# A decoder layer on one core: the last 32 prompt tokens of the first half move from the row gathers to the dense expert products, and three early products move behind the gates' table

## The chip, the cores and the metric

The kernel runs on one core of a Trainium2 chip. The metric is the device time of one execution in microseconds (us); the median of three timed runs stands for the kernel.

## What is computed

One decoder layer for a prompt of 1024 tokens and 8 sample sequences of 4 tokens, which share all weights. The mixer (a state-space scan and dilated window attention) and the first norm are not touched by the change. What follows them is:

```
h   = LayerNorm1(ALPHA * x + m)
out = LayerNorm2(ALPHA * h + PEER(h))

qh  = h @ w_q                               # 8 heads, two halves of 128 each
s1, s2 = qh[:128] @ keys_1.T, qh[128:] @ keys_2.T
top 16 of s1, top 16 of s2, then the top 16 of their sums  -> 128 experts e of 16384, gates g
hid = gelu(u_tab[e] . h)
out = sum over the 128 experts of g * hid * v_tab[e]
```

Each token uses 128 of 16384 experts; each of the tables u and v holds 16384 rows of 1024 numbers (64 MB).

## The kernel before

**Two ways to the experts.** The prompt is worked through in two halves of 512 tokens (`PARTS`, line 36); the 32 sample tokens go with the first half through the mixer. The experts are then computed in two ways that run beside each other:

- *By row.* The 512 tokens of the first half (`TD`, line 37) lie in four tiles of 128 tokens. For each tile, each of the two tables and each of the 128 chosen experts, `gathers` (line 1851) fetches one row per token with an indirect DMA that POOL issues (line 1866, 128 rows of 4 KB), and VectorE (DVE) multiplies it: line 1892 for u (a dot product with the token), line 1897 for v (an accumulation into a bank pair of PSUM). That makes 1024 such steps. Six row buffers are in use and the fetch runs five steps ahead (`ROWS, LOOK`, line 66). A tile ends with its norm (`norm2`, line 1905), two loads of the norm's vectors, two POOL instructions and a store.
- *Dense.* For the 512 tokens of the second half and the 32 sample tokens (`TE` = 544, line 38) `dense` (line 1674) computes all 16384 experts: 128 products with u (a "hidden" product: gelu, then the gate is multiplied in) and 128 with v (an "output" product, added to the result). Expert rows come in 16 blocks `c` of 8 products `k`, per block first the 8 hidden ones, then the 8 output ones. A product is a `step` (line 431) of 48 matmuls: 8 pieces of the depth, three part products each (high by high, low by high, high by low part of 32-bit numbers), and two column pieces `TPC` (line 62), here 288 and 256 wide. Each product takes 0.5 MB of weights, loaded in two halves by SP, split by ScalarE (ACT, line 370) and POOL or DVE (line 371) two products ahead.

**The gates' table.** The dense way needs the gate of each (expert, token) pair. `gates` (line 1596) builds it four tokens at a time: DVE compares (line 1631), POOL multiplies (line 1633), PE does four 128x128 products (line 1640), ACT copies the result out of PSUM (line 1650), and SP stores 32 tokens at once to DRAM (line 1652). The table of 544 tokens takes 136 such groups. The 32 sample tokens come first: their experts are known already (`given`, line 1602). The other four tiles wait until the choice of experts for the second half (the lane `top`, DVE work in `route`) is done; the first of them then runs its `choose` on DVE and POOL in one go (lines 1665 to 1669).

**The order of the work** is written out by hand. A product calls `tick` a set number of times, and at each tick every lane (the choice of experts, the gates' table, the gathers) advances by its rate, so that its instructions stand between those of the products on each engine. 16 hidden products (`BEFORE`, line 93: the eight of block 0 and two each of blocks 1 to 4) are computed early, while the table is built, with `EARLY` ticks each (line 89); those of blocks 1 to 4 are parked in DRAM (line 1721) from two buffers `er` and fetched back later. In this stretch the gathers advance by `GATHERT` = 0.2 steps per tick. All 16 use the same PSUM room, so that each waits for the gelu of the one before.

After the 16 products the table's lane is finished off, its memory is closed, SP loads the first two pieces of the table (`table`, line 1687; issued in line 1694), and DVE multiplies the gates in (`weigh`, line 1701). The other 240 products follow with `DTICKS` = 4 ticks each; the steps by row that are left are spread evenly over them (line 1823). The last two products run one column piece after the other, and the norm of the dense tokens (`cnorm`, line 1291) ends the kernel.

Of the kernel before, what the change touches and what calls it, by code (L numbers as in the profile page):

```python
# [7 lines left out]
F32 = mybir.dt.float32  # L8
# [3 lines left out]
AF = mybir.ActivationFunctionType  # L12
ALU = mybir.AluOpType
# [6 lines left out]
NB = 8  # L20
# [12 lines left out]

PARTS = [(0, 512, True), (512, 512, False)]
TD, PD = PARTS[-1][:2]
TE = PD + NS
NTG = TD // 128
NPAIR = 50  # L40
PACK = NE * NE
# [44 lines left out]
NLO = "vpvpvpvp"  # L86


EQ, OBUFS, EARLY = 4, 4, [8] + [9] * 13 + [4] * 2


AHEAD = {1: 2, 2: 2, 3: 2, 4: 2}
BEFORE = [(0, 0, k) for k in range(8)] + [(c, 0, k) for c in AHEAD for k in range(AHEAD[c])]
STEPS = [s for s in ((c, half, k) for c in range(NE // 8) for half in range(2) for k in range(8)) if s not in BEFORE]


# [45 lines left out]
def layout(inp):  # L142
# [59 lines left out]


OUTS = {
    "y": (TD, D),
    "y1": (128, 8, TE),
    "pk": (128, 4, SEQ + NS),
    "pv": (128, 4, SEQ + NS),
# [9 lines left out]
def unlayout(r):  # L218
    y = r["y"]
    y1 = r["y1"].transpose(2, 1, 0).reshape(TE, D)  # L220
    yp = np.concatenate([y, y1[:PD]])

    def tok(m):
        return m.transpose(2, 1, 0).reshape(-1, 8, 64)

    k, v = tok(r["pk"]), tok(r["pv"])

    def cache(old, new):
        return np.concatenate([old.reshape(NB, PAST - NL, 8, 64), new[SEQ:].reshape(NB, NL, 8, 64)], 1)[None]

    out = (
        yp[None], y1[PD:].reshape(NB, NL, D),
        k[:SEQ][None, None], v[:SEQ][None, None],
        r["pconv"].transpose(2, 1, 0).reshape(1, 1, 3, 2560),
        r["pssm"].T.reshape(1, 1, NH, 64, 128),
        cache(r["sk"], k), cache(r["sv"], v),
        r["sconv_o"].transpose(2, 3, 1, 0).reshape(1, NB, 3, 2560),
        r["sssm_o"].transpose(1, 0, 3, 2).reshape(1, NB, NH, 64, 128),
    )
    return tuple(np.ascontiguousarray(o) for o in out)  # L240
# [15 lines left out]
class Build:  # L256
# [40 lines left out]
    def run(self):  # L297
        nc, t = self.nc, self.t
        cp = self.open("const")
        self.wp = self.open("w", 3)  # L300
        self.P = self.open("psum", space=PSUM).tile([128, 8, 512], F32, name="P")
        dpool = self.wdram = self.open("dram", space=DRAM)
        self.cst = cp.tile([128, C_N], F32, name="cst")
        self.convw = cp.tile([128, 20, 5], F32, name="convw")
        self.chans = cp.tile([128, 56], F32, name="chans")
        self.heads = cp.tile([128, 2, 24], F32, name="heads")
        self.keys = cp.tile([128, 2, 128], F32, name="keys")
        self.eps = cp.tile([128, 1], F32, name="eps")
        self.ctail = cp.tile([128, 20, 3], F32, name="ctail")
        self.ecol = [cp.tile([128, 128], I32, name=f"ecol{i}") for i in range(NTG)]  # L310
        self.gate = [cp.tile([128, 128], F32, name=f"gate{i}") for i in range(NTG)]
        self.smp_e = cp.tile([NS, 128], I32, name="smpe")
        self.smp_g = cp.tile([NS, 128], F32, name="smpg")
        self.hd = [dpool.tile([128, D], F32, name=f"hd{i}") for i in range(NTG)]
        self.kd = [dpool.tile([128, 4, n], F32, name=f"kd{i}") for i, (_, n, _) in enumerate(PARTS[:-1])]
        self.vd = [dpool.tile([128, n // 128, 512], F32, name=f"vd{i}") for i, (_, n, _) in enumerate(PARTS[:-1])]
        self.hx = dpool.tile([128, 8, NS], F32, name="hx")
        self.ssm = dpool.tile([128, NH * 64], F32, name="ssm")
        self.ed = {(c, k): dpool.tile([128, TE], F32, name=f"ed{c}{k}") for c in AHEAD for k in range(AHEAD[c])}
        self.gd = dpool.tile([TE // 32, 128, NE, 32], F32, name="gd")  # L320
        self.gen = self.gathers()
        self.pumping, self.seat, self.chosen = None, None, 0
        self.weights()
        with self.tc.manual_schedule():
            self.start()
            for i in range(len(PARTS)):
                self.part(i)
            nc.sync.dma_start(t["pconv"], self.ctail)
            self.dense()
        self.close("g", "hh", "dram", "psum", "w", "const")  # L330
# [844 lines left out]
    def third(self, hf):  # L1175
# [101 lines left out]
        if not self.last:  # L1277
            for k in range(8):
                if NLO[k] == "v":
                    nc.scalar.activation(self.r[:, k], self.r[:, k], AF.Identity, bias=self.chans[:, 32 + k:33 + k])  # L1280
            if self.smp:
                nc.sync.dma_start(self.hx, self.r[:, :, self.PT:])
        else:
            sp = self.open(f"n{hf}", side="right")
            hx = sp.tile([128, 8, NS], F32, name="hx", tag="hx", bufs=1)
            nc.sync.dma_start(hx, self.hx)
            self.split(self.h[0][:, :, T:], self.h[1][:, :, T:], hx, nc.gpsimd)
            self.close(f"n{hf}")
# [87 lines left out]
    def route(self, hf, first):  # L1376
# [10 lines left out]
        self.routed = self.tiles[:n], self.best, self.sbest if self.smp else None  # L1387
        held = SCORES[hf]
        if self.last:
            others = [self.lane(self.experts(sp, (self.smp_e, self.smp_g), NS, self.given))]  # L1390
        else:
            if not hf:
                self.gp = self.open("g")
            self.xrp = sp
            others = [self.lane(self.rows(sp), 0.5), self.lane(self.inputs(hf + 1), 0.25)]
# [62 lines left out]
    def pairs_room(self, n):  # L1458
        pool = self.open("best", side="right")
        if self.smp:  # L1460

            self.sbest = [pool.tile([128, 1, 2, TK], d, name=f"sbest{i}") for i, d in enumerate((F32, U32, F32))]
        if self.last:
            self.given = pool.tile([128, 3, 128], F32, name="eT")
        return [pool.tile([128, n, PH, TK], d, name=f"best{i}") for i, d in enumerate((F32, U32, F32))]

    def pairs(self, sp, keys, best, h0):
# [128 lines left out]
    def gates(self, sp):  # L1596
# [1 line left out]
        nc = self.nc  # L1598
        tiles, (sv, si, pk), _ = self.routed

        work = [(NS, PD)] + list((m, s) for s, m in tiles)
        given = 1
        groups = [(w, t) for w in range(len(work)) for t in range(0, work[w][0], 4)]
        eTs, o12, sts, outs, cp = {0: self.given}, {}, {}, {}, {}

        iota = self.bank(6)[:, 384:]
        nc.scalar.activation(iota, self.c(C_IOTE), AF.Copy)
# [34 lines left out]
        def store(q):  # L1642
            if q < 0:
                return
            w, t0 = groups[q]
            at = work[w][1] + t0
# [11 lines left out]
        for q in range(len(groups)):  # L1658
            w, t0 = groups[q]
            mults(q)  # L1660
            store(q - 1)
            if t0 == 0 and w < len(work) - 1:
                gen = experts(w + 1)
            next(gen, 0)
            if t0 == work[w][0] - 4 * OBUFS:
                while w < given and self.top.live:
                    yield
                for _ in gen:
                    pass
            build(q + OBUFS - 1)  # L1670
            yield
        store(len(groups) - 1)

    def dense(self):
# [41 lines left out]

        def early(c, k, ps):
            if c:
                row = sp.tile([128, n], F32, name="er", tag="er", bufs=2)
                gelu(row, ps)  # L1720
                nc.sync.dma_start(self.ed[c, k], row)
            else:
# [84 lines left out]
        table_lane = self.lane(self.gates(sp))  # L1807
        table_lane.run()
        for i, (c, _, k) in enumerate(BEFORE):
            product(4, hs, EARLY[i], lambda ps, c=c, k=k: early(c, k, ps))  # L1810
            self.settle()
        self.settle(table_lane)
        self.close("ga", "gc", "best")
        dp = self.open("dn", 2)
        for i in range(2):
            table(0, i)
        self.settle()
        for k in range(9):
            if k < 8:
                weigh(0, k, r[:, k])  # L1820
# [30 lines left out]
    def gathers(self):  # L1851
# [6 lines left out]
        def fetch(k):  # L1858

            while ahead[0] <= min(k, len(plan) - 1) and plan[ahead[0]][0] < self.chosen:  # L1860
                k0, (gi, tab, s) = ahead[0], plan[ahead[0]]
                if tab == s == 0:
                    heads[gi] = gp.tile([128, D], F32, name="gh", tag="gh")
                    nc.sync.dma_start(heads[gi], self.hd[gi])
                rows[k0] = gp.tile([128, D], F32, name="row", tag="row", bufs=ROWS)
                nc.gpsimd.indirect_dma_start(out=rows[k0], out_offset=None, in_=t["uv"[tab]],  # L1866
                                             in_offset=bass.IndirectOffsetOnAxis(ap=self.ecol[gi][:, s:s + 1], axis=0))
                ahead[0] += 1

        def seat(dst, src, scale=1.0):  # L1870
# [4 lines left out]
        for k, (gi, tab, s) in enumerate(plan):  # L1875
            while ahead[0] <= k:
                fetch(k)
                yield
            hs = heads[gi]
            if s == 0:  # L1880
                if tab == 0:
                    hid = gp.tile([128, 128], F32, name="hid", tag="hid")
# [6 lines left out]
                at, moved = seat(self.seat, at), True  # L1889
            r = rows.pop(k)  # L1890
            if tab == 0:
                nc.vector.scalar_tensor_tensor(r, r, 1.0, at, op0=ALU.mult, op1=ALU.mult, accum_out=hid[:, s:s + 1])  # L1892
                if s == 127:
                    nc.scalar.activation(hid, hid, AF.Gelu)
                    nc.vector.tensor_tensor(hid, hid, self.gate[gi], op=ALU.mult)
            else:
                nc.vector.scalar_tensor_tensor(at, r, hid[:, s:s + 1], at, op0=ALU.mult, op1=ALU.add)  # L1897
                if s == 127:
                    acc = seat(gp.tile([128, D], F32, name="acc", tag="acc"), at) if moved else at
                    self.norm2(acc, t["y"][gi * 128:gi * 128 + 128], 128)  # L1900
            fetch(k + LOOK)
            self.left -= 1
            yield
# [34 lines left out]
```

## Time and profile before

| | us |
|---|---|
| median of 3 timed runs (3718.92 to 3726.46) | 3719.44 |
| the profiled execution, its own time | 3715.19 |
| its span, first to last instruction | 3713.3 |
| choice of experts ends, gates' table with early products (about) | 1792 to 2070 |
| three more early products, load of the table's first pieces | 2070 to 2112 |
| 240 dense products with the gathers beside them | 2112 to 3683 |
| end: norm of the dense tokens | 3683 to 3713 |

The page's busy share counts a matmul from its start to its modelled end, and they overlap; how far PE is from its own pace is read from the start times of neighbouring matmuls and from its idle times. [...] The DMA share is the mean busy share of the 16 DMA engines and can pass 1.00 a little.

### The profile page before, as it was taken

How to read it: one execution, taken by the hardware profiler on the slowest of the kernel's cores; microseconds unless marked ns; L12 is line 12 of the kernel's file. 1: busy time of each engine (PE TensorE's matmuls, PEld its weight loads, DVE VectorE, ACT ScalarE, POOL GpSimd, SP SyncE). 2: the span in 40 equal slices, each digit the busy share in tenths (PEclk: the TensorE clock that was granted, in tenths of full speed). 3: DMA queues.
4: the chain of work that ended last, by engine and by line, in shares of the span. 5: the costliest groups of instructions: out<-in, count | busy, mean ns of one | idle time of the engine just before them, and what ended most of it. 6: DMA issues, size and time to landing. Idle time of an engine off the chain costs nothing. (4 is left out here: it accounts for less than half of the span.)

```text
span 3713.3 us, 62101 instructions
## 1 busy us (share of the span) xinstructions
PE 3310.6 (89%) x22560; PEld 2972.8 (80%) x22560; DVE 2711.9 (73%) x5565; ACT 1176.9 (32%) x2178; POOL 2336.3 (63%) x2250
## 2 busy tenths in 40 slices
PE   7999999989798778779488799999899999899998
PEld 6757778988566566567488799999899999899997
DVE  2325654379777998759899587888787788788886
ACT  3423224342333222221266422222222223222223
POOL 4303555333465667630488688888788887888885
PEclk9999999999899899889799899999999999999999
DMA  7665447996568867964156799999999999999995
GB/s 248 195 209 187 146 148 237 375 337 213 180 196 303 301 221 271 371 247 148 63 216 251 254 378 367 371 368 371 345 381 376 370 366 354 351 373 368 375 375 189
DMA packets 464658, 1057.77 MB, mean 285 GB/s; under 512 B 49632, under 2 KB 152544, under 8 KB 461664
## 3 DMA queue, kind: packets, MB, share of 16 engines
q1 hardware_dynamic: 316896, 516.88, 40.6%
q0 software_dynamic: 147456, 536.94, 38.8%
q8 instruction: 177, 2.90, 0.3%
q14 instruction: 129, 1.06, 0.1%
HBM read 910.59 MB, written 172.11 MB: 292 GB/s over the span
## 5 line engine op out<-in xcount | busy, mean ns | idle before, releaser
L371 POOL TENSOR_TENSOR wlo<-wraw,whi 128x512 fp32r<-128x512 f32 x524 | 679.9, 1303 | 348.3 <-ACT whi L370 313.0
L1897 DVE SCALAR_TENSOR_TENSOR P<-row,hid,P 128x1024 f32<-128x1024 f32 x512 | 657.9, 1285 | 130.5 <-DMA row<-in_v,ecol 120.9
L370 ACT ACTIVATE whi<-wraw 128x512 fp32r<-128x512 f32 (+1 forms) x668 | 410.1, 627 | 973.3 <-DMA wraw<-in_vd 396.0
L450 PE MATMUL P<-hh,whi 128*128 128x288 f32 (+3 forms) x2648 | 632.4, 304 | 44.2 <-DVE al L1707 23.3
L1866 POOL DMA_INDIRECT row<-in_u,ecol x512 | 517.9, 1012 | 218.0 <-DVE row L1892 88.9
L450 PE MATMUL P<-hh,wlo 128*128 128x288 f32 (+3 forms) x2648 | 625.2, 301 | 10.7 <-POOL wlo L371 5.8
L450 PE MATMUL P<-hl,whi 128*128 128x288 f32 (+3 forms) x2648 | 626.8, 302 | 2.8 <-POOL hl L1322 2.5
L1892 DVE SCALAR_TENSOR_TENSOR row<-row,P 128x1024 f32<-128x1024 f32 x440 | 526.9, 1215 | 137.3 <-DMA row<-in_u,ecol 112.7
L1866 POOL DMA_INDIRECT row<-in_v,ecol x512 | 496.4, 970 | 173.4 <-issue 69.9
L450 PEld LDWEIGHTS P<-hh,whi 128*128 128x128 f32 x2648 | 437.6, 194 | 59.6 <-DVE al L1707 16.6
L450 PE MATMUL P<-xh,whi 128*128 128x272 f32 (+4 forms) x1288 | 436.4, 349 | 44.1 <-ACT xr L740 20.1
L450 PEld LDWEIGHTS P<-hh,wlo 128*128 128x128 f32 x2648 | 436.8, 193 | 21.3 <-DMA wlo<-ws 6.7
L450 PEld LDWEIGHTS P<-hl,whi 128*128 128x128 f32 x2648 | 437.9, 194 | 12.1 <-POOL hl L1322 3.8
L450 PE MATMUL P<-xl,whi 128*128 128x272 f32 (+4 forms) x1288 | 422.1, 338 | 7.9 <-POOL xl L371 7.5
L450 PE MATMUL P<-xh,wlo 128*128 128x272 f32 (+4 forms) x1288 | 420.1, 336 | 4.4 <-DMA wlo<-ws 4.4
L450 PE MATMUL P<-ah,whi 128*128 128x288 f32 (+1 forms) x1536 | 328.0, 293 | 25.2 <-DVE r L1743 25.1
L450 PE MATMUL P<-ah,wlo 128*128 128x288 f32 (+1 forms) x1536 | 326.5, 293 | 15.0 <-POOL wlo L371 15.0
L450 PE MATMUL P<-al,whi 128*128 128x288 f32 (+1 forms) x1536 | 325.1, 292 | 0.0
L450 PEld LDWEIGHTS P<-xh,whi 128*128 128x128 f32 (+1 forms) x1288 | 248.6, 197 | 77.6 <-ACT xr L740 22.1
L450 PEld LDWEIGHTS P<-xl,whi 128*128 128x128 f32 (+1 forms) x1288 | 248.5, 197 | 34.8 <-POOL xl L371 9.6
L450 PEld LDWEIGHTS P<-xh,wlo 128*128 128x128 f32 (+1 forms) x1288 | 247.4, 196 | 32.2 <-DMA wlo<-ws 6.6
L371 DVE TENSOR_TENSOR wlo<-wraw,whi 128x512 fp32r<-128x512 f32 (+1 forms) x144 | 144.9, 1007 | 167.6 <-ACT whi L370 139.4
(382 smaller groups left out, 5816.7 us busy)
## 6 DMA issues: line engine op xcount, KB each, us to landing
wraw<-in_ut SPq DMA_DIRECT2D x256, 256.0 KB, 6.0
wraw<-in_vd SPq DMA_DIRECT2D x256, 256.0 KB, 5.6
ws<-whi SPq DMA_DIRECT2D x152, 256.0 KB, 4.4
ws<-wlo SPq DMA_DIRECT2D x152, 256.0 KB, 4.8
whi<-ws SPq DMA_DIRECT2D x152, 256.0 KB, 6.6
wlo<-ws SPq DMA_DIRECT2D x152, 256.0 KB, 4.9
gd<-gst SPq DMA_DIRECT2D x17, 2048.0 KB, 8.5
g<-gd SPq DMA_DIRECT2D x90, 256.0 KB, 11.6
```

Of the source, the lines that this page charges most:

```text
L370: nc.scalar.activation(hi, src, AF.Copy)
L371: (eng or nc.vector).tensor_tensor(lo, src, hi.bitcast(F32), op=ALU.subtract)
L450: nc.tensor.matmul(outs[i], w[a][:, k, :m], x[b][k][:, s:s + n], start=first and st, stop=last and sp)
L1866: nc.gpsimd.indirect_dma_start(out=rows[k0], out_offset=None, in_=t["uv"[tab]], in_offset=bass.IndirectOffsetOnAxis(ap=self.ecol[gi][:, s: ...
L1892: nc.vector.scalar_tensor_tensor(r, r, 1.0, at, op0=ALU.mult, op1=ALU.mult, accum_out=hid[:, s:s + 1])
L1897: nc.vector.scalar_tensor_tensor(at, r, hid[:, s:s + 1], at, op0=ALU.mult, op1=ALU.add)
```

## The change

32 tokens (`EXTRA`), the last of the first half, are taken from the steps by row and given to the dense way. There are now 480 tokens by row, in four tiles of which the last has 96 tokens, and 576 dense ones: 32 extra, 32 sample, 512 of the second half. Both column pieces are 288 wide; the table has 18 blocks of 32 tokens and 144 groups. The experts of the 32 extra tokens are known from the first half, so that their eight groups stand behind those of the sample tokens and before the wait for `top` (`given` = 2).

Of the 16 early products, 13 now run while the table is built, with more ticks each (8, eleven times 10, 11), in the order: five of block 0, the eight of blocks 1 to 4, and then, behind the end of the table and the issue of the first two table loads, the last three of block 0. The buffers `er` go from two to one.

```diff
+EXTRA = 32
 TD, PD = PARTS[-1][:2]
-TE = PD + NS
+TG = TD - EXTRA
+NX = EXTRA + NS
+TE = PD + NX
...
-EQ, OBUFS, EARLY = 4, 4, [8] + [9] * 13 + [4] * 2
+EQ, OBUFS, EARLY = 4, 4, [8] + [10] * 11 + [11]
...
-BEFORE = [(0, 0, k) for k in range(8)] + [(c, 0, k) for c in AHEAD for k in range(AHEAD[c])]
+BEFORE = [(0, 0, k) for k in range(5)] + [(c, 0, k) for c in AHEAD for k in range(AHEAD[c])] + [(0, 0, k) for k in range(5, 8)]
...
-            others = [self.lane(self.experts(sp, (self.smp_e, self.smp_g), NS, self.given))]
+            others = [self.lane(self.experts(sp, *v)) for v in zip(((self.smp_e, self.smp_g), (self.ecol[-1], self.gate[-1])), (NS, 128), self.given)]
...
-        work = [(NS, PD)] + list((m, s) for s, m in tiles)
-        given = 1
-        groups = [(w, t) for w in range(len(work)) for t in range(0, work[w][0], 4)]
-        eTs, o12, sts, outs, cp = {0: self.given}, {}, {}, {}, {}
+        work = [(NS, PD + EXTRA, 0), (EXTRA, PD, 128 - EXTRA)] + [(m, s, 0) for s, m in tiles]
+        given = 2
+        groups = [(w, t) for w in range(len(work)) for t in range(work[w][2], work[w][2] + work[w][0], 4)]
+        eTs, o12, sts, outs, cp = dict(enumerate(self.given)), {}, {}, {}, {}
...
-            if t0 == 0 and w < len(work) - 1:
+            if t0 == work[w][2] and given - 1 <= w < len(work) - 1:
                 gen = experts(w + 1)
             next(gen, 0)
-            if t0 == work[w][0] - 4 * OBUFS:
-                while w < given and self.top.live:
+            if t0 == work[w][2] + work[w][0] - 4 * OBUFS:
+                while w == given - 1 and self.top.live:
                     yield
...
-                row = sp.tile([128, n], F32, name="er", tag="er", bufs=2)
+                row = sp.tile([128, n], F32, name="er", tag="er", bufs=1)
...
         for i, (c, _, k) in enumerate(BEFORE):
-            product(4, hs, EARLY[i], lambda ps, c=c, k=k: early(c, k, ps))
+            if i == len(EARLY):
+                self.settle(table_lane)
+                self.close("ga", "gc", "best")
+                dp = self.open("dn", 2)
+                for j in range(2):
+                    table(0, j)
+            product(4, hs, EARLY[i] if i < len(EARLY) else DTICKS, lambda ps, c=c, k=k: early(c, k, ps))
             self.settle()
-        self.settle(table_lane)
-        self.close("ga", "gc", "best")
-        dp = self.open("dn", 2)
-        for i in range(2):
-            table(0, i)
-        self.settle()
...
-                rows[k0] = gp.tile([128, D], F32, name="row", tag="row", bufs=ROWS)
+                m = min(128, TG - gi * 128)
+                rows[k0] = gp.tile([128, D], F32, name="row", tag="row", bufs=ROWS)[:m]
                 nc.gpsimd.indirect_dma_start(out=rows[k0], out_offset=None, in_=t["uv"[tab]],
-                                             in_offset=bass.IndirectOffsetOnAxis(ap=self.ecol[gi][:, s:s + 1], axis=0))
+                                             in_offset=bass.IndirectOffsetOnAxis(ap=self.ecol[gi][:m, s:s + 1], axis=0))
```

The DVE and ACT instructions of the last tile's steps by row get `[:m]` as well (96 instead of 128 partitions, the same number of elements in each); the copy of the sample tokens' columns that goes through DRAM (`hx`) has 64 columns instead of 32.

## Rows read from the trace of the kernel before

**Rows 1.** Busy time by stretch: us, engines (instructions), then granted clock, DMA share, GB/s
```profile
1792.00:2070.00 278.00, 218.94 (x1716) 211.84 (x1717) 252.43 (x369) 166.59 (x180) 221.42 (x206) 0.91 0.56 203
2070.00:2112.00 42.00, 19.91 (x150) 18.93 (x149) 10.44 (x16) 11.96 (x18) 14.91 (x11) 0.81 0.81 277
2112.00:3683.00 1571.00, 1490.45 (x11476) 1475.97 (x11475) 1261.86 (x1619) 431.80 (x734) 1291.96 (x1183) 0.97 0.98 360
...
3059.00:3107.00 48.00, 48.00 (x385) 48.00 (x384) 41.92 (x41) 17.05 (x30) 41.11 (x38) 1.00 1.01 374
...
2296.00:2348.00 52.00, 50.04 (x385) 49.85 (x384) 37.82 (x65) 11.24 (x19) 41.80 (x40) 0.97 1.03 379
```

**Rows 2.** Timeline of PE in the last two products: start, duration, instruction
```profile
3676.19 0.29 PE L450 MATMUL P<-ah,whi 128*128 128x288 f32 x1
...
3682.45 0.29 PE L450 MATMUL P<-ah,wlo 128*128 128x288 f32 x1
...
3684.55 0.28 PE L450 MATMUL P<-al,whi 128*128 128x256 f32 x1
...
3686.68 0.28 PE L450 MATMUL P<-al,whi 128*128 128x256 f32 x1
```

**Rows 3.** Who waited for whom, PE, 2112 to 3683: us in total, times, longest
```profile
PE P L450 <- DVE r L1743: 28.9, 17, 5.8
PE P L450 <- DVE al L1707: 23.3, 13, 3.7
PE P L450 <- POOL wlo L371: 20.8, 8, 10.1
```

**Rows 4.** The same for DVE in that stretch
```profile
DVE row L1892 <- DMA row<-in_u,ecol: 109.6, 117, 3.4
DVE P L1897 <- DMA row<-in_v,ecol: 94.0, 107, 3.4
```

**Rows 5.** DVE groups in that stretch: count, busy us, mean ns, idle before
```profile
L1897 DVE SCALAR_TENSOR_TENSOR P<-row,hid,P 128x1024 f32<-128x1024 f32 x384 | 493.5, 1285 | 101.1 <-DMA row<-in_v,ecol 94.0 <-ACT P L1871 1.6 <-ACT P L1697 0.4
L1892 DVE SCALAR_TENSOR_TENSOR row<-row,P 128x1024 f32<-128x1024 f32 x381 | 456.8, 1215 | 134.2 <-DMA row<-in_u,ecol 109.6 <-POOL wlo L371 10.5 <-issue 8.8
...
L1701 DVE TENSOR_TENSOR P<-P,g 128x544 f32<-128x544 f32 x112 | 81.3, 726 | 12.9 <-ACT P L1697 12.9
```

**Rows 6.** DMA queue of the gathers, whole span: packets, MB, share of 16 engines
```profile
q0 software_dynamic: 147456, 536.94, 38.8%
```

**Rows 7.** DVE while the table is built, 1850 to 2110
```profile
L1631 DVE TENSOR_TENSOR oo<-P,eT 128x1024 f32<-128x1024 f32 x123 | 144.1, 1214 | 5.5 <-PE P L1592 2.1 <-PE P L1640 1.6 <-ACT eT L1594 1.3
```

**Rows 8.** Timeline of DVE behind the choice of experts: idle before in brackets
```profile
1822.57 0.69 DVE L1542 TENSOR_REDUCE zz<-ez 128x32 f32<-128x512 f32 x1 [2.03 <-ACT ez L1540]
...
1834.52 1.22 DVE L1574 TENSOR_REDUCE ef<-eq 128x64 f32<-128x1024 f32 x1 [2.52 <-POOL eq L1571]
```

**Rows 9.** Timelines of SP, ACT and PE around the end of the table
```profile
2070.28 0.33 SPq L1652 DMA_DIRECT2D gd<-gst  x1
...
2102.80 12.12 SPq L1694 DMA_DIRECT2D g<-gd  x3
...
2070.51 0.62 ACT L1697 ACTIVATE er<-P 128x544 f32<-128x544 f32 x1 [0.26 <-PE P L450]
...
2093.98 0.62 ACT L1697 ACTIVATE er<-P 128x544 f32<-128x544 f32 x1 [5.39 <-PE P L450]
...
2111.40 0.82 PE L1793 MATMUL P<-ah,whi 128*128 128x288 f32 x2 [17.51 <-ACT ah L1704]
```

**Rows 10.** What SP's queue waited for, 2060 to 2125
```profile
SPq L1919 <- POOL acc L1918: 10.6, 1, 10.6
...
SPq L1694 <- DMA ed<-er: 4.7, 1, 4.7
```

**Rows 11.** End of the chain that ended last: norm of the 288, then of the 256 columns
```profile
3695.00 1.95 DVE g L1131
...
3704.24 1.76 DVE g L1131
```

More of the change, by code (lines that the diff above doesn't have):

```diff
@@ L204 @@
 OUTS = {
-    "y": (TD, D),
+    "y": (TG, D),
     "y1": (128, 8, TE),
@@ L220, in unlayout @@
     y1 = r["y1"].transpose(2, 1, 0).reshape(TE, D)
-    yp = np.concatenate([y, y1[:PD]])
+    yp = np.concatenate([y, y1[PD:PD + EXTRA], y1[:PD]])
     def tok(m):
@@ L231, in unlayout @@
     out = (
-        yp[None], y1[PD:].reshape(NB, NL, D),
+        yp[None], y1[PD + EXTRA:].reshape(NB, NL, D),
         k[:SEQ][None, None], v[:SEQ][None, None],
@@ L316, in run @@
         self.vd = [dpool.tile([128, n // 128, 512], F32, name=f"vd{i}") for i, (_, n, _) in enumerate(PARTS[:-1])]
-        self.hx = dpool.tile([128, 8, NS], F32, name="hx")
+        self.hx = dpool.tile([128, 8, NX], F32, name="hx")
         self.ssm = dpool.tile([128, NH * 64], F32, name="ssm")
@@ L1281, in third @@
             if self.smp:
-                nc.sync.dma_start(self.hx, self.r[:, :, self.PT:])
+                nc.sync.dma_start(self.hx, self.r[:, :, self.PT - EXTRA:])
         else:
             sp = self.open(f"n{hf}", side="right")
-            hx = sp.tile([128, 8, NS], F32, name="hx", tag="hx", bufs=1)
+            hx = sp.tile([128, 8, NX], F32, name="hx", tag="hx", bufs=1)
             nc.sync.dma_start(hx, self.hx)
@@ L1463, in pairs_room @@
         if self.last:
-            self.given = pool.tile([128, 3, 128], F32, name="eT")
+            self.given = [pool.tile([128, 3, 128], F32, name=f"eT{i}") for i in range(2)]
         return [pool.tile([128, n, PH, TK], d, name=f"best{i}") for i, d in enumerate((F32, U32, F32))]
@@ L1645, in store @@
             w, t0 = groups[q]
-            at = work[w][1] + t0
+            at = work[w][1] + t0 - work[w][2]
             if at % 32 == 0:
@@ L1878, in gathers @@
                 yield
-            hs = heads[gi]
+            hs, m = heads[gi], min(128, TG - gi * 128)
             if s == 0:
@@ L1891, in gathers @@
             if tab == 0:
-                nc.vector.scalar_tensor_tensor(r, r, 1.0, at, op0=ALU.mult, op1=ALU.mult, accum_out=hid[:, s:s + 1])
+                nc.vector.scalar_tensor_tensor(r, r, 1.0, at[:m], op0=ALU.mult, op1=ALU.mult, accum_out=hid[:m, s:s + 1])
                 if s == 127:
-                    nc.scalar.activation(hid, hid, AF.Gelu)
-                    nc.vector.tensor_tensor(hid, hid, self.gate[gi], op=ALU.mult)
+                    nc.scalar.activation(hid[:m], hid[:m], AF.Gelu)
+                    nc.vector.tensor_tensor(hid[:m], hid[:m], self.gate[gi][:m], op=ALU.mult)
             else:
-                nc.vector.scalar_tensor_tensor(at, r, hid[:, s:s + 1], at, op0=ALU.mult, op1=ALU.add)
+                nc.vector.scalar_tensor_tensor(at[:m], r, hid[:m, s:s + 1], at[:m], op0=ALU.mult, op1=ALU.add)
                 if s == 127:
                     acc = seat(gp.tile([128, D], F32, name="acc", tag="acc"), at) if moved else at
-                    self.norm2(acc, t["y"][gi * 128:gi * 128 + 128], 128)
+                    self.norm2(acc[:m], t["y"][gi * 128:gi * 128 + m], m)
             fetch(k + LOOK)
```

## Prediction

> **What bounds the kernel now.** I read the table of busy time by stretch first. From 2112 to 3683 the 240 dense products run beside the gathers: 1571 us, 42% of the span, 6.55 us a product, with TensorE (PE), the DMAs and, less so, DVE nearly full [rows 1]. Busy time can't say which of them bounds, so I went on to the start times of neighbouring matmuls [rows 2]: between 3676.19 and 3682.45 lie 47 steps of 288 columns, 133 ns each; between 3684.55 and 3686.68 lie 18 of 256 columns, 118 ns each. A product of 24 pairs thus needs 24 x 251 ns = 6.02 us, and 240 need 1446 us. The stretch 3059 to 3107, eight hidden products in 48.0 us, shows that PE can keep this pace beside the gathers; the next kind, eight output products from 2296 to 2348, needs 52 us [rows 1]. So the stage lies 125 us above PE's own pace.
>
> The list of waits says what these 125 us are. PE waits for DVE (the sum into the result, the low part of the gated hidden values) and for one POOL split: 73 us [rows 3]. The rest is mostly the clock: 0.97 over the stage means that some 3% of it, 45 us, is lost to half speed [rows 1], which falls behind the longer waits. And DVE itself waits 204 us for gathered rows, in 224 waits of up to 3.4 us [rows 4]. The chain is: rows arrive late, DVE is late, PE waits. One product moves 360 GB/s x 6.55 us = 2.36 MB [rows 1]; at PE's own pace that would be 392 GB/s, more than the 374 to 379 GB/s of the stretches shown [rows 1]. **The dense stage is bound by the DMAs, with PE 8% behind.**
>
> **The change, part by part.**
>
> *Dense products.* 5760 second pieces grow from 256 to 288 columns, 15 ns each [rows 2]: +86 us of PE work. PE's own pace becomes 24 x 266 ns = 6.39 us a product, 1533 us for 240. [...]
>
> *DVE, ACT, POOL in it.* Instructions over all dense tokens grow by 6%: on DVE a hidden product has two of about 0.72 us and an output product one [rows 5], so +0.06 us a product; with 1262 of 1571 us busy [rows 1] it is covered by DVE's own 204 us of waiting. If that cover goes, it is worth 16 us.
>
> *Gathers.* 765 of the 1024 steps by row (384 + 381) fall into this stage [rows 5], the last tile's 256 into its last third, about 76 products. All gathers move 536.94 MB in 1024 steps, 0.52 MB each [rows 6]; the last tile's lose a quarter, 34 MB in all. Their DVE instructions have as many elements per partition as before; no row shows one on 96 partitions, so between no gain and a quarter of 256 x 1.25 us, 80 us, in a third of the stage where DVE won't be the bound: I take none. So for the first 164 products DMA demand is unchanged (2.36 MB; a few KB more of table) and PE slower: 2.36 / 6.39 = 369 GB/s, under the 379 seen. For the last 76 it is 1.95 / 6.39 = 305 GB/s. PE becomes the bound in both. What stays above PE's pace: today 125 us, of which I put 34 us on two tile ends inside the stage (the POOL wait of 10.1 us [rows 3], and the half clock around both) and 6 on its start; 85 us, 0.36 a product, is the late rows. I take a third of it, 0.12, where demand is still 97% of what was seen (20 us), and 0.03 for the last third (2 us). Bounds: nothing, as from 3059 to 3107, and the full 0.36. Sum: 1533 + 34 + 22 = 1589, **+18 us** (-4 to +60).
>
> *The table.* Eight more groups, each 1.21 us on DVE [rows 7], +9.7 us in a stage where DVE is busy 252 of 278 us [rows 1]. The ticks fit: the table needs about 146, the 13 products give 129 and two more each while their gelu is settled, 155. At 0.2 steps a tick, one or two more steps by row fall in here (+1.5 us, taken from the dense stage). Against it, the choice of the first tile no longer runs bare: today DVE waits for ACT 2.03 and for POOL twice 2.52 us [rows 8], and the extra groups stand beside the first of these. **+9 us** (3 to 14); the longer matmuls of the 13 products lie under DVE.
>
> *The three products behind the table.* Today the table's last store is issued at 2070.28, just when the thirteenth product's gelu starts (2070.51), and three products follow in 7.0 us each; but the load of the table's first pieces is issued only at 2102.80, so PE stands 17.5 us until 2111.40 [rows 9]. That load waits on SP behind a tile end's store (10.6 us) and for the parked products' landing (4.7 us) [rows 10]. Afterwards the table ends near 2079 and the thirteenth product, with some eight ticks left, near 2084. Three products of 6.39 and 0.9 us each for the gelu between them end near 2106. The load is queued ahead of them; it waits for the last parked product, is issued near 2094 and lands about 8 us later, so DVE can multiply the gates in before PE needs them. PE goes on near 2106.5 instead of 2111.4: **-5 us** with the table's +9 in it (-12 to +4). What is queued behind the waiting load on SP are weight halves for products two further on: one product's time of slack, the upper bound's reason. The start lag of 6 us in the dense stage (half clock, gates just in time) goes; it is in the 1589.
>
> *The rest.* Two extra small DVE conversions and a transpose in the choice of experts, +1. In the end norm the second piece is as wide as the first: 1.95 instead of 1.76 us for the same instruction [rows 11], over some 17 us with parts that don't grow: +1.5. `hx` is one small copy: 0.
>
> **Sum:** 18 - 5 + 2.5 = +15 us on the execution profiled, 3715.2 to 3731. The timed median lies 4.2 above that execution, so about 3734. A difference of 0.2% (7.4 us) is about what a measurement can tell.
>
> **The rivals.**
>
> 1. *PE becomes the only bound (faster).* With PE at 6.39 us the rows have 6% more time, DVE is never late, long waits and with them the half clock vanish. The hidden stretch at full pace beside 374 GB/s [rows 1] speaks for it; against it that DVE and its row waits fill nearly the whole stage (1262 + 204 of 1571). It decides from where late rows cost under 0.03 us a product. Dense 1533 + 34 = 1567 (-4), handover -10 with the load never in the way, +2.5: 3719 - 12 = 3707. [...]
>
> 2. *Late rows keep their price (much slower).* If the 0.36 us a product comes from the six row buffers' round trip and not from bandwidth, it stays on top of the slower PE in the first 164 products: 59 instead of 20 us, and 3719 + 15 + 39 = 3773. For it: 224 short waits, spread evenly [rows 4]; against it: output products, which also load the table, are the slow ones [rows 1].
>
> 3. *The small gather brings nothing.* If 96 rows take as long as 128, the last 76 products pay 0.12 as well: +7, 3741. No row has a gather of another size.
>
> 4. *The handover turns.* If the load's wait on SP makes weights late, PE stands some 8 us behind the table and restarts at half clock: 3746.
>
> **How the numbers follow.** Forecast 0.46, spread 3722 to 3750; rival 1 0.26; rival 2 0.12; rival 3 0.06; rival 4 0.10. Faster by over 0.2%: most of rival 1, 0.22. Within 0.2%: its upper edge and the lower quarter of the forecast, 0.23. Slower: 0.55. The range 3704 to 3762 leaves out rival 2 and the edge of rival 1.
>
> **What would show it.** In the changed profile matmuls of the dense stage start 133 ns apart throughout; the stage takes about 1589 us; DVE's waits for rows fall from 204 us to under 150 and nearly vanish in the last 500 us; GB/s fall to about 305 there; PE's gap before the first output product is under 3 us instead of 17.5; the table's last store comes near 2079. Wrong it would be if PE still waited 70 us for DVE and POOL (rival 2), or if the stage ended under 1575 us (rival 1).

## The result: 3.5% slower, and where the time went

The kernel with the change takes 3848.37 us (median of four runs, 3836.23 to 3866.62), the kernel before beside it 3719.18 (3715.49 to 3726.46): a ratio of 1.0349, 95% interval 1.0305 to 1.0393. The forecast was 3734, its range 3704 to 3762. The profiled execution of the changed kernel is the slowest of the four, 3866.62 us, with a span of 3864.9; some 18 us of what follows are this execution's own. Line numbers are 4 or 5 higher than before: the matmuls stand in L454 and L1797, the steps by row in L1897 and L1902.

Busy time by stretch, changed kernel. The columns are those of [rows 1] (the engines stand in the order PE, PE's weight loads, DVE, ACT, POOL; a granted clock of 1.00 is TensorE's full speed); the stretches are the dense stage up to the last tile of rows, the last tile (96 tokens), and the rest:

```profile
2128.00:3187.00 1059.00, 1026.90 (x7597) 1022.06 (x7597) 857.38 (x1077) 289.97 (x487) 852.80 (x782) 0.99 0.99 357
3187.00:3800.00 613.00, 530.59 (x3686) 517.98 (x3684) 401.52 (x518) 142.51 (x238) 408.59 (x387) 0.94 1.03 248
3800.00:3865.00 65.00, 46.90 (x276) 42.37 (x276) 33.49 (x51) 20.92 (x38) 21.56 (x15) 0.86 0.30 91
```

The same three stretches in the kernel before:

```profile
2112.00:3148.00 1036.00, 988.14 (x7605) 977.65 (x7604) 843.13 (x1082) 286.20 (x485) 851.66 (x782) 0.97 1.00 365
3148.00:3657.00 509.00, 480.28 (x3714) 476.51 (x3713) 410.96 (x525) 139.73 (x240) 423.50 (x390) 0.97 0.99 364
3657.00:3713.00 56.00, 39.37 (x241) 35.15 (x239) 25.72 (x45) 18.70 (x35) 16.81 (x12) 0.86 0.24 83
```

The 152 us between the spans are 16 ahead of the stage, 23 in the two full tiles, **104 in the last tile** and 9 at the end. Even most of those 9 belong to the last tile: its last step by row ends at 3808.4, 3657.9 before, so that to its last step it takes 621 us instead of 510, and the end behind it 56.5 instead of 55.4. The last tile is the odd one: the DMAs are busy all the time (1.03), but move 248 GB/s instead of 364. The tile whose rows were cut by a quarter has become the slow one.

In the full tiles PE is the bound, as foreseen. The timeline of PE over two of their products (each row holds two matmuls, and the second row shown is the 48th after the first) shows 12.80 us for 96 matmuls, 133 ns each, as for 288 columns in [rows 2]:

```profile
2707.50 0.43 PE L454 MATMUL P<-hh,wlo 128*128 128x288 f32 x2
...
2720.30 0.43 PE L454 MATMUL P<-hh,wlo 128*128 128x288 f32 x2
```

Who waited for whom: PE in the full tiles, against [rows 3]:

```profile
PE P L454 <- DVE al L1711: 9.9, 7, 3.2
PE P L454 <- POOL wlo L375: 9.8, 1, 9.8
PE P L454 <- DVE r L1747: 9.2, 5, 3.4
```

and PE in the last tile, then ACT (the split of the weights) there, and ACT in the last tile of before:

```profile
PE P L454 <- DVE al L1711: 26.8, 13, 10.5
PE P L454 <- POOL wlo L375: 16.2, 12, 11.5
PE P L454 <- ACT whi L374: 14.9, 6, 4.1
PE P L454 <- DVE r L1747: 12.5, 8, 2.5
...
ACT whi L374 <- DMA wraw<-in_ut: 158.3, 46, 12.8
ACT whi L374 <- DMA wraw<-in_vd: 137.8, 44, 11.8
...
ACT whi L370 <- DMA wraw<-in_ut: 111.9, 37, 13.8
ACT whi L370 <- DMA wraw<-in_vd: 104.2, 35, 7.6
```

In the full tiles PE waits 29 us in 1059. In the last tile it waits 70 us in 613 for work that hangs on the weights and the rows, and the clock falls to 0.94 with it. Not the gathers alone are late, but the weight loads too: ACT stands 296 us for them, against 216 before, and PE now waits for ACT's split as well (14.9 us).

DVE's waits for rows, against [rows 4], full tiles first, then the last one:

```profile
DVE row L1897 <- DMA row<-in_u,ecol: 67.9, 61, 3.1
DVE P L1902 <- DMA row<-in_v,ecol: 58.7, 73, 2.6
...
DVE row L1897 <- DMA row<-in_u,ecol: 82.7, 72, 10.6
DVE P L1902 <- DMA row<-in_v,ecol: 81.2, 80, 6.4
```

The queue of the gathers, against [rows 6]: 33.6 MB fewer, and not a bit less time, since 38.8% of a longer span is more of it:

```profile
q0 software_dynamic: 139264, 503.38, 38.8%
```

The steps by row on DVE, against [rows 5], now on 96 partitions. They take as long as on 128:

```profile
L1902 DVE SCALAR_TENSOR_TENSOR P<-row,hid,P 96x1024 f32<-96x1024 f32 x123 | 157.8, 1283 | 83.0 <-DMA row<-in_v,ecol 81.2 <-ACT P L1876 0.6 <-DVE r L1747 0.3
L1897 DVE SCALAR_TENSOR_TENSOR row<-row,P 96x1024 f32<-96x1024 f32 x128 | 154.3, 1214 | 85.7 <-DMA row<-in_u,ecol 82.7 <-ACT P L1876 1.9 <-issue 0.6
```

The end of the table, against [rows 9]: timelines of SP, of ACT and of PE (start, duration; idle before in brackets):

```profile
2087.34 0.32 SPq L1656 DMA_DIRECT2D gd<-gst  x1
...
2102.82 0.34 SPq L1924 DMA_DIRECT2D out_y<-acc  x1
2103.26 0.51 SPq L413 DMA_DIRECT2D wraw<-in_vd  x1
2103.82 0.66 SPq L1725 DMA_DIRECT2D ed<-er  x1
2109.70 6.13 SPq L1698 DMA_DIRECT2D g<-gd  x2
2115.89 5.25 SPq L413 DMA_DIRECT2D wraw<-in_vd  x1
...
2125.73 1.22 ACT L374 ACTIVATE whi<-wraw 128x512 fp32r<-128x512 f32 x2 [16.83 <-DMA wraw<-in_vd]
2126.86 0.63 ACT L1701 ACTIVATE r<-P 128x576 f32<-128x576 f32 x1
...
2128.11 0.85 PE L1797 MATMUL P<-ah,whi 128*128 128x288 f32 x2 [12.49 <-ACT ah L1708]
```

and what SP waited for there, against [rows 10]:

```profile
SPq L1924 <- POOL acc L1923: 13.4, 1, 13.4
SPq L1698 <- DMA ed<-er: 5.1, 1, 5.1
```

The table's last store comes 17 us later than before and the first output product 16.7 us later. The load of the table still stands on SP behind the tile end's store and the parked product's landing, and now a weight load stands behind it (2115.89). ACT waits for those weights, and the third gelu behind the table, whose matmuls end near 2115.6, stands in line behind ACT's split until 2126.86. PE still waits 12.5 us.

### The profile page after: what moved, and what is told of

Its sections match the earlier page's. It is cut to its first block, busy times and chain, and to the rows that moved or that the text cites. A ratio compares the mean times of both kernels' runs of the same rounds, so it can differ in the third digit from the quotient of the medians.

```text
span 3864.9 us, 62291 instructions
## 1 busy us (share of the span) xinstructions
PE 3428.2 (89%) x22627; PEld 3083.9 (80%) x22627; DVE 2741.5 (71%) x5576; ACT 1194.7 (31%) x2188; POOL 2340.3 (61%) x2258
## 3 DMA queue, kind: packets, MB, share of 16 engines
q0 software_dynamic: 139264, 503.38, 38.8%
## 4 chain that ended last, share of the span: by engine, by line
PE 27%; DVE 19%; DMA 18%; POOL 11%; issue 7%; ACT 2%; SPq 0%; POOLq 0%; DVEq 0%; ACTq 0%
PE P L454 20%; DMA row<-in_v,ecol 5%; POOL row L1871 4%; DMA wraw<-in_vd 4%; DMA wraw<-in_ut 3%; POOL wlo L375 3%; DVE row L1897 3%; DMA row<-in_u,ecol 2%; DMA wlo<-ws 2%; DVE P L1902 2%; POOL oo L1637 2%; PE P L1797 2%; DVE cv L758 1%; DVE oo L1635 1%; PE P L719 1%
## 5 line engine op out<-in xcount | busy, mean ns | idle before, releaser
L1902 DVE SCALAR_TENSOR_TENSOR P<-row,hid,P 128x1024 f32<-128x1024 f32 (+1 forms) x512 | 657.4, 1284 | 178.0 <-DMA row<-in_v,ecol 167.9
L454 PE MATMUL P<-hh,whi 128*128 128x288 f32 (+3 forms) x2648 | 654.0, 312 | 68.8 <-DVE al L1711 36.7
L1897 DVE SCALAR_TENSOR_TENSOR row<-row,P 128x1024 f32<-128x1024 f32 (+1 forms) x440 | 526.5, 1214 | 182.3 <-DMA row<-in_u,ecol 166.9
L454 PE MATMUL P<-hl,whi 128*128 128x288 f32 (+3 forms) x2648 | 646.0, 309 | 3.1 <-POOL hl L1326 2.9
L454 PE MATMUL P<-hh,wlo 128*128 128x288 f32 (+3 forms) x2648 | 641.3, 309 | 7.4 <-DMA wlo<-ws 4.1
L454 PEld LDWEIGHTS P<-hh,whi 128*128 128x128 f32 x2648 | 455.1, 195 | 87.3 <-DVE al L1711 31.3
L454 PE MATMUL P<-xh,whi 128*128 128x272 f32 (+4 forms) x1288 | 435.3, 348 | 47.3 <-ACT xr L744 20.9
L454 PEld LDWEIGHTS P<-hh,wlo 128*128 128x128 f32 x2648 | 453.8, 194 | 18.9 <-DMA wlo<-ws 5.5
L454 PEld LDWEIGHTS P<-hl,whi 128*128 128x128 f32 x2648 | 454.8, 194 | 12.7 <-POOL hl L1326 4.2
L454 PE MATMUL P<-xl,whi 128*128 128x272 f32 (+4 forms) x1288 | 421.4, 337 | 7.9 <-POOL xl L375 7.5
L454 PE MATMUL P<-xh,wlo 128*128 128x272 f32 (+4 forms) x1288 | 419.1, 336 | 3.8 <-DMA wlo<-ws 3.7
L454 PE MATMUL P<-ah,whi 128*128 128x288 f32 x1536 | 339.5, 301 | 25.8 <-DVE r L1747 21.6
L454 PE MATMUL P<-ah,wlo 128*128 128x288 f32 x1536 | 339.1, 301 | 25.4 <-POOL wlo L375 25.4
L454 PE MATMUL P<-al,whi 128*128 128x288 f32 x1536 | 337.5, 300 | 0.0
L454 PEld LDWEIGHTS P<-xh,whi 128*128 128x128 f32 (+1 forms) x1288 | 248.1, 197 | 80.7 <-ACT xr L744 22.9
L454 PEld LDWEIGHTS P<-xl,whi 128*128 128x128 f32 (+1 forms) x1288 | 247.9, 197 | 34.6 <-POOL xl L375 9.5
L454 PEld LDWEIGHTS P<-ah,whi 128*128 128x128 f32 x1536 | 252.7, 193 | 28.5 <-issue 18.2
```

The costliest lines, as they stand in the source:

```text
L454: nc.tensor.matmul(outs[i], w[a][:, k, :m], x[b][k][:, s:s + n], start=first and st, stop=last and sp)
L1897: nc.vector.scalar_tensor_tensor(r, r, 1.0, at[:m], op0=ALU.mult, op1=ALU.mult, accum_out=hid[:m, s:s + 1])
L1902: nc.vector.scalar_tensor_tensor(at[:m], r, hid[:m, s:s + 1], at[:m], op0=ALU.mult, op1=ALU.add)
```

## The experiments

Each time is a median, its ratio one to the kernel before in the same runs. The packets' durations were read from the trace's DMA records, from 3200 or 3250 us on, within the last tile, and stand in the same form throughout: 4096 bytes is a gathered row, 2048 bytes a weight packet, 512 bytes one of the gates' table.

### All 128 rows fetched, 96 used

```diff
-                m = min(128, TG - gi * 128)
+                m = 128 if gi < NTG - 1 else 128
...
-            r = rows.pop(k)
+            r = rows.pop(k)[:m]
```

> The changed kernel, but the last tile fetches 128 rows a step again and uses 96 of them; its output is the same. Theory A (a gather is slow when its rows don't fall to the DMA engines in eights; 96 = 16 x 6) and theory B (a gather of fewer than 128 rows is slow as such) both expect the last tile's products back from 7.98 us to about 6.45 us, 115 us less: near 3735 us, packets of 4096 bytes back from 265 to 170 ns, and 360 GB/s or more in the last third. Theory C (the last tile is slow for another reason, weights or DVE) expects no change, 3848 us.

3738.19 us (3732.97 to 3747.85), ratio 1.0054 (1.0033 to 1.0076): 110 us come back by fetching more, with DVE's steps still on 96 partitions. Busy time from 3200 to 3600 in the kernel before:

```profile
3200.00:3600.00 400.00, 386.81 (x3022) 383.90 (x3020) 326.59 (x425) 108.97 (x188) 335.08 (x313) 0.99 1.01 373
```

in the changed one:

```profile
3200.00:3600.00 400.00, 352.79 (x2472) 345.49 (x2472) 262.61 (x382) 91.15 (x151) 269.43 (x257) 0.95 1.03 253
```

and in this one:

```profile
3200.00:3600.00 400.00, 394.37 (x2941) 393.50 (x2940) 321.58 (x427) 112.92 (x191) 331.09 (x308) 1.00 1.00 367
```

```
median packet, ns     4096 B   2048 B   512 B
before                  160      84      27
changed, 96 rows        262     134      36
this, 128 rows          160      84      27
```

The same DMA time carries 253 GB/s or 367. And packets of all three sizes are slow beside a 96-row gather, also the weights', which go to all 128 partitions (134 against 84 ns). The changed kernel itself has the other half of the comparison: in its two full tiles (2200 to 3100) the medians are 159, 84 and 27 ns. What is left of the change costs 0.5%.

### 120 and 112 rows

The same edit with 120 and with 112 rows; the compute uses 96:

```diff
-                m = min(128, TG - gi * 128)
+                m = 128 if gi < NTG - 1 else 120
```

> The same with 120 rows fetched in the last tile (96 used). Theory A: 120 is 15 x 8, so this is as fast as with 128 rows, near 3735 us, packets of 4096 bytes near 170 ns. Theory B: a quarter of the loss is left (8 of the 32 missing rows), some 3765 us, packets near 190 ns. [...]

> The same with 112 rows fetched in the last tile (96 used). Theory A: 112 is 16 x 7, so it is slow although it has only 8 rows fewer than the run with 120: between 3780 and 3850 us, packets of 4096 bytes over 200 ns. Theory B: half of the loss, some 3790 us, packets near 215 ns. What tells the theories apart is the step between 120 and 112 rows: over 45 us by A, some 25 us by B.

3957.50 us (ratio 1.0633, 1.0614 to 1.0651) and 3894.24 us (1.0468, 1.0450 to 1.0486). Median packets of 4096 bytes take 262 and 252 ns, of 2048 bytes 133 and 127.

Both theories fall in the form in which they were expected. Rows in whole eights don't help, 120 and 112 are both slow (how their rows divide over the DMA engines was the author's assumption, no run shows it); and the loss doesn't go with the missing rows, since 120, the nearest to 128, is the worst of all. Packed gathers of 96, 112 and 120 rows pay about the same per row (262, 252 and 262 ns), so more rows only cost more. With 120 rows a gather also leaves more 4-byte packets on its queue: 18432 in the whole execution, which are 16 for each of 768 full gathers and 24 for each of the 256 of 120 rows. With 96 and with 112 rows there are 16384, or 16 for every gather.

### 64 rows, packed or at every second partition

In the last tile a step gathers 64 rows, to partitions 0 to 63, and DVE and ACT use a single partition of them, so that the output of this tile's tokens is left out:

```diff
-                m = min(128, TG - gi * 128)
-                rows[k0] = gp.tile([128, D], F32, name="row", tag="row", bufs=ROWS)[:m]
-                nc.gpsimd.indirect_dma_start(out=rows[k0], out_offset=None, in_=t["uv"[tab]],
+                m = slice(0, 128) if gi < NTG - 1 else slice(0, 64)
+                rows[k0] = gp.tile([128, D], F32, name="row", tag="row", bufs=ROWS)
+                nc.gpsimd.indirect_dma_start(out=rows[k0][m], out_offset=None, in_=t["uv"[tab]],
...
-            r = rows.pop(k)
+            u = 128 if gi < NTG - 1 else 1
+            r = rows.pop(k)[:u]
```

and the spread one beside it, with the same 64 indices, to tell whether the number of rows makes a gather slow or the place where they land:

```diff
-                m = slice(0, 128) if gi < NTG - 1 else slice(0, 64)
+                m = slice(0, 128) if gi < NTG - 1 else slice(0, 128, 2)
```

> The changed kernel with 64 rows fetched a step in the last tile, into partitions 0 to 63; the steps of that tile compute with the first partition alone (the same number of instructions and of elements in each), so y of the last 96 rows is left out. 120 rows were slower than 112, and 112 slower than 96, so the split into eights is not what decides by the number of rows. [...] With 64 rows the bytes are so few that the time may still be near 3750 us; the packets tell.

> [...]

Packed 3792.63 us (two runs, 3786.08 and 3799.18; 1.0194, 1.0168 to 1.0220), spread 3728.24 us (eight runs, 3723.62 to 3737.47; 1.0023, 1.0010 to 1.0035): **the same number of rows and bytes, 64 us apart by the place where they land.** From 3200 to 3600, packed:

```profile
3200.00:3600.00 400.00, 372.66 (x2692) 368.67 (x2692) 295.88 (x409) 107.92 (x180) 294.18 (x283) 0.97 1.04 216
```

and spread:

```profile
3200.00:3600.00 400.00, 400.00 (x3002) 400.00 (x3002) 327.03 (x433) 111.02 (x192) 332.53 (x318) 1.00 0.78 245
```

```
median packet, ns     4096 B   2048 B   512 B
64 packed               312     151      40
64 spread               159      84      27
```

Packed, half the rows still fill the DMAs (1.04). Spread, they leave them a fifth of their time, and PE runs without a gap. The median hides a tail, though: one in ten of the spread rows' packets takes over 300 ns, and their mean is 199 ns, where it is 172 before.

The spread run answers a second question. Even with the last tile at PE's own pace, the time from the first output product (2123.41) to the end of the span (3723.1) is 1599.7 us, against 3713.3 - 2111.4 = 1601.9 before. 288 columns in both pieces set a floor that eats what the gathers give, and the start, 12 us later, is left as a loss.

### 32 rows at three spacings

The 64-row edit again (one partition used, the tile's output left out), with 32 indices and the slice below, then `slice(0, 96, 3)`, then `slice(0, 32)`:

```diff
-                m = slice(0, 128) if gi < NTG - 1 else slice(0, 128, 2)
+                m = slice(0, 128) if gi < NTG - 1 else slice(0, 128, 4)
```

> The changed kernel, whose last tile gathers 32 rows per step to every fourth partition (0 to 124); the tile's own compute uses one partition only, so the output of its tokens is left out. [...]

> [...] Theory F: the cost goes with the part of the range that is not covered, a quarter here as in the 96-row gather, where packets took 262 ns; so slow as well, but no slower than there. Theory G (only neighbouring partitions in one gather collide, any stride of two or more is free): 160 and 84 ns, the time of stride 4.

> The same 32 rows per step as at strides 3 and 4, but packed into partitions 0 to 31; the tile's own compute uses one partition only, so the output of its tokens is left out. The load is that of the two runs before, some 0.6 of the DMAs' time. [...]

3729.75 us (1.0021, 1.0010 to 1.0032), 3735.59 (1.0025, 1.0014 to 1.0037) and 3731.49 (1.0027, 1.0012 to 1.0043). With so few rows PE is the bound in all three, and the times can't tell them apart; the DMAs' share for the same bytes does. From 3200 to 3600, stride 4:

```profile
3200.00:3600.00 400.00, 400.00 (x3003) 400.00 (x3002) 325.69 (x433) 109.98 (x191) 325.32 (x318) 1.00 0.59 177
```

stride 3:

```profile
3200.00:3600.00 400.00, 400.00 (x3003) 400.00 (x3002) 326.98 (x445) 113.26 (x194) 324.80 (x318) 1.00 0.60 177
```

packed:

```profile
3200.00:3600.00 400.00, 400.00 (x3002) 400.00 (x3002) 326.93 (x442) 112.92 (x195) 323.55 (x318) 1.00 0.66 176
```

```
mean (median), ns     4096 B        512 B
stride 4              196 (159)     27.6 (27)
stride 3              209 (159)     29.8 (27)
packed                236 (198)     36.6 (29)
```

Stride 3 is as fast as stride 4 in the median (159 ns, where theory G had 160), 13 ns slower in the mean. Packed is slow in part of its packets: 198 ns in the median and 236 in the mean, against 159 and 196 at stride 4. So rows packed close cost something even here. Packets that are slow throughout stand only in the runs with full DMAs (shares of 1.03 and 1.04); whether the load or the number of rows makes that difference is not shown, since no run has 32 packed rows and full DMAs. The theory that what counts is how much of the range of partitions is covered falls twice: 120 rows cover nearly all of it and are slow (262 ns), stride 3 leaves a quarter out and is not (159 ns).

### The new order without the 32 tokens, and the 32 tokens without it

The kernel before with the change's `EARLY`, `BEFORE`, one `er` buffer and the table's loads in front of the last three early products:

```diff
-EQ, OBUFS, EARLY = 4, 4, [8] + [9] * 13 + [4] * 2
+EQ, OBUFS, EARLY = 4, 4, [8] + [10] * 11 + [11]
...
+            if i == len(EARLY):
+                self.settle(table_lane)
+                self.close("ga", "gc", "best")
+                dp = self.open("dn", 2)
+                for j in range(2):
+                    table(0, j)
...
```

and the changed kernel with this undone: the old order, the table's loads behind all sixteen, one `er` buffer:

```diff
-EQ, OBUFS, EARLY = 4, 4, [8] + [10] * 11 + [11]
+EQ, OBUFS, EARLY = 4, 4, [8] + [9] * 13 + [4] * 2
...
```

> The kernel before with the other part of the change alone: 544 dense tokens and 512 by row as before, but three early products behind the end of the table and the loads of its first pieces ahead of them. My forecast for that part was a gain of 5 to 12 us at the handover: 3707 to 3714 us, and PE's gap before the first output product under 3 us instead of 17.5. The rival, that the loads' wait on SP holds up weights and with them the gelu on ACT, expects a gap of 10 us or more and 3719 to 3730 us.

> The changed kernel with the old order and ticks of the 16 early products (all before the table's close, loads behind them), one er buffer. The order alone changed nothing with 544 tokens (3722 against 3721 us), so by that 3848 us again, within 15. If the new order hides something only together with the longer table, 3860 us or more; if it costs, under 3835 us.

3722.34 us, ratio 1.0006 (0.9995 to 1.0016), and 3847.87, ratio 1.0352 (1.0329 to 1.0374) against 1.0349 for the whole change. The order is worth nothing with either table. Why, the timelines of SP, ACT and PE in the run with 544 dense tokens say:

```profile
2093.72 6.84 SPq L1694 DMA_DIRECT2D g<-gd  x2
2100.68 6.15 SPq L409 DMA_DIRECT2D wraw<-in_vd  x1
...
2111.20 1.22 ACT L370 ACTIVATE whi<-wraw 128x512 fp32r<-128x512 f32 x2 [14.19 <-DMA wraw<-in_vd]
2112.32 0.61 ACT L1697 ACTIVATE r<-P 128x544 f32<-128x544 f32 x1
...
2113.53 0.82 PE L1793 MATMUL P<-ah,whi 128*128 128x288 f32 x2 [10.21 <-ACT ah L1704]
```

The two loads of the table hold SP from 2093.72 to past 2100, the weights behind them come late, ACT's split waits 14.2 us for them, and the gelu that PE needs stands behind the split. The old wait has moved from the table's load to the weights behind it.

### The table's loads one and two products later

In the kernel before with the new order, each of the two loads goes one product further back:

```diff
-                for j in range(2):
-                    table(0, j)
+            if i > len(EARLY):
+                table(0, i - len(EARLY) - 1)
```

> The run with the order alone (544 dense tokens, 512 by row), but the two table loads are issued one and two products later, so that no weight load stands behind their wait for the parked products on SP. If that wait and the loads' own traffic ahead of the weights are what gave the gain back (ACT stood 14.2 us for weights, with the last gelu and the first high part queued behind it), PE's gap before the first output product falls from 10.2 to under 5 us and the time to 3712 to 3717 us. The rival, that the tile end's store (11.9 us on SP) delays everything behind it anyway, expects 3719 to 3725 us.

3714.89 us (12 runs, 3709.12 to 3725.33), ratio 0.9985 (0.9974 to 0.9997): 0.15% faster than the kernel before, which the interval just separates from nothing, and the lowest median of all. SP, ACT and PE again:

```profile
2096.04 0.38 SPq L1694 DMA_DIRECT2D g<-gd  x1
2097.06 4.35 SPq L409 DMA_DIRECT2D wraw<-in_vd  x2
2101.46 0.43 SPq L1694 DMA_DIRECT2D g<-gd  x1
...
2104.81 0.62 ACT L1697 ACTIVATE r<-P 128x544 f32<-128x544 f32 x1 [5.16 <-PE P L450]
...
2107.83 0.52 PE L1793 MATMUL P<-ah,whi 128*128 128x288 f32 x2 [3.06 <-ACT ah L1704]
```

Weights now go between the two loads, the gelu follows its own matmuls, and PE's gap is 3.1 us. The output products start 3.6 us earlier than before [rows 9]. The gain is small, and this profiled execution (3720.83 us) doesn't show it, being 6 us above its kernel's median.

One more step, 0.25 instead of 0.2 steps by row per tick, so that the first tile's norm ends ahead of the table's end:

```diff
-GATHER, GATHERT = [[0, 0, 0, 0], [4, 4.2, 3.5, 0.0]], 0.2
+GATHER, GATHERT = [[0, 0, 0, 0], [4, 4.2, 3.5, 0.0]], 0.25
```

> The kernel before with the new order and the table's two loads one product apart (the run with 3714.9 us), and 0.25 instead of 0.2 steps by row per tick while the table is built, so that the norm of the first tile comes earlier and its store does not stand on SP in front of the loads. If the 12 us that SP waits for that norm are what the end of the table still costs: 5 to 8 us under the kernel before. If nothing waits for these loads any more: 3712 to 3718, as without it. If DVE, busy nine tenths of the table's stage, pays for the steps: as the kernel before, 3717 to 3723.

3733.25 us, ratio 1.0024 (1.0012 to 1.0035): slower than any of the expectations allowed, against 3724.41 for the kernel before in these runs. The norm's store and the table's last store on SP:

```profile
2055.29 0.34 SPq L1919 DMA_DIRECT2D out_y<-acc  x1
...
2087.87 0.32 SPq L1652 DMA_DIRECT2D gd<-gst  x1
```

and the norm's instructions on POOL:

```profile
2050.49 4.77 POOL L1918 TENSOR_TENSOR acc<-acc,lng 128x1024 f32<-128x1024 f32 x2 [7.80 <-DMA lng<-in_ln]
```

The norm did come earlier, and the table's end 17 us later (2087.87 against 2070.99 with 0.2). Part of that is DVE, which is busy 252 of 278 us there [rows 1]: by its last comparison for the table it has done 34 steps by row, where it had done 27 with 0.2, and the norm. The rest is POOL, which none of the expectations had: it waits 7.8 us for the norm's vectors, loaded only when the tile ends, and works 4.8 us at the norm, and the table's multiplications stand behind that. PE waits 9.9 us for them and DVE 7.7. The same load is what the tile end's store waits for in [rows 10]: POOL stands 10.7 us for it in the kernel before and 12.0 in the changed one. A run that loads the vectors earlier is missing.

## Why the prediction was wrong

**The step that failed is "Gathers".** It took 34 MB off the last tile, divided what was left by PE's pace and had "for the last 76 it is 1.95 / 6.39 = 305 GB/s. PE becomes the bound in both". That prices a gather of 96 rows by its bytes at the rate of 128-row gathers. Measured: 248 GB/s with the DMAs full, packets of 262 instead of 160 ns, and 621 us for the last tile, to its last step. The forecast's own terms give it 76 x 6.39 + 2 + 17 for its end (half of the 34) = 505 us, about the 510 of before. The text did bound the small gather, but from one side only: rival 3, "the small gather brings nothing", let it cost as much as 128 rows and no more. The bound on the other side, that fewer rows could take longer, was missing, and so the range ended at 3762. The full 0.36 us a product was laid on the first 164 products only; on all 240 (1533 + 34 + 86, so +82 instead of +18) it gives 3798, still 50 us short. Nothing in the trace of before excluded it: there was no gather of another size.

**The rest of the dense term held.** With 128 rows fetched, the kernel is what rival 3 describes: 3741 there, 3738.19 measured. PE's step of 133 ns, the 6.4 us a product, DVE's 96-partition steps without a gain (1283 and 1214 ns) came as written. One sign did not: DVE's waits for rows were to fall under 150 us in all, and in the full tiles alone they are 127 us, against 72.7 + 64.7 = 137 us in the same stretch of before. The rows are as late as they were; PE, slower, no longer waits behind them. **Rival 1** put the dense stage at -4; with the last tile wholly at PE's pace, 64 rows spread, it is -2 with the end norm in it. Its other 10 us were the handover's, which did not come. **Rival 2**'s 3773 lies nearer to the result, but by chance: its late rows were to show in the full tiles, where PE waits 29 us. The sign named for it, 70 us of waiting for DVE and POOL, did come (84 us), but 56 of them stand in the last tile.

**The handover was wrong too.** "The three products behind the table" gave -5 us with the table's +9 in it; the first output product starts 16.7 us later in the changed kernel and 10.7 later with 128 rows (2122.07 against 2111.40). Of that, the table's last store is 17.1 and 10.1 us later (2087.34 and 2080.41 against 2070.28), of which +9 was foreseen; the two kernels are the same up to there, so the 7 us between them are the executions' own. The three products behind the table were read as 7.0 us each in [rows 9]; from 2070.51 to 2093.98 they are 7.8 in the mean, since a tile's end stands beside the first. The gain of the new order, put at some 14 us, was zero, as the order alone showed. The forecast knew that weights were queued behind the waiting load, gave them "one product's time of slack" and left the turn to **rival 4**. That is what happened, by the mechanism named there: 16.8 us of ACT's waiting, a gelu behind it, PE standing 12.5. With 128 rows this error hides: the start is 16 us worse than forecast (+10.7 for -5) and the rest 20 us better (+7 for rival 3's 25 and 2.5), so that 3738 beside 3741 is partly luck.

**The end norm** grew about as said: +1.5 was forecast, the stretch behind the last step by row is 1.1 us longer, and both halves are now at the longer price of [rows 11]:

```profile
3846.74 1.95 DVE g L1135
...
3855.52 1.96 DVE g L1135
```

## What to carry to other kernels

A gather's price is not its bytes (here 96 rows a step moved 248 GB/s with the DMAs full, 128 rows 364): before a tile is cut below 128 partitions, time one such gather beside the traffic it will have, or keep 128 rows and throw some away. Where rows must be fewer, spread them over the partitions at an even stride (64 rows: 159 instead of 312 ns for the median packet). And when a load is moved up in the order in which one engine issues its loads, look at what stands behind it, and put it between the loads that the next products need rather than in front of them (PE's gap was 10.2 us with both loads in front, 3.1 with weights between them).

## What the runs showed of the hardware

Where they fill the DMAs, gathers into fewer than 128 packed partitions slowed the whole DMA traffic of the core in these runs: the median packet of a row takes 1.6 times as long at 96, 112 and 120 rows (262, 252 and 262 against 160 ns) and 1.95 times at 64 (312 ns), and weight packets that go to all partitions take 1.5 to 1.8 times as long (127 to 151 against 84 ns). The same 64 rows at every second partition leave the medians at 159 and 84 ns, and PE without a gap: they move 245 GB/s at a DMA share of 0.78, the packed ones 216 at 1.04.

At a lighter load, 32 packed rows a step (share 0.66) are slowed less than 64: 198 ns in the median, against 159 at strides 3 and 4 (0.60 and 0.59). No run here shows which engine wrote which partition, and the cause within the DMAs stays open. Why 120 rows leave 24 packets of 4 bytes a gather, where 96, 112 and 128 rows leave 16, is open as well.
